# Rotary embedding on one core: casting loads and stores alternate in one ring, as DMAs of every fourth row

## Chip, core and metric

The kernel runs on 1 core of one Trainium2 chip. The metric is device time in microseconds (us), the median of several executions of the whole program. The profile is of one such execution.

## What is computed

The kernel rotates the two halves of every attention head by a position-dependent angle. x is float32 of 16 batches x 512 positions x 1024 values (16 heads of 64); cos and sin are float32 of 512 x 32.

```python
x = x.reshape(batch, seq, num_heads, head_dim)
x1, x2 = x[..., :half_dim], x[..., half_dim:]
cos = cos[None, :, None, :]
sin = sin[None, :, None, :]
rotated = np.concatenate([
    x1 * cos - x2 * sin,
    x1 * sin + x2 * cos
], axis=-1)
```

The result is float32 of the same size as x: 33.55 MB are read and 33.55 MB written.

## The kernel before

One batch is one unit of work: 512 positions x 1024 values, laid out as 128 partitions (rows of the tile) x 4096 values. Each partition holds four consecutive positions, which are contiguous in HBM, so a row is one run of 16 KB in float32. There are 16 batches, and for each the loop (L74 on) does four things.

- Load (L45 for the first three batches, L79 for the others): one DMA of 2 MB brings the batch to a float32 tile `xt`. It is issued on SP, on the queue that the profile calls hardware_dynamic. `xpool` has 4 buffers, so a load waits until ACT has cast the batch four before.
- Cast (L84): ACT copies `xt` to `xb` in bf16, 128x4096 in one instruction.
- Products and sum (L101, L102, L109): for each of the four positions of a partition, VectorE (DVE) multiplies `xb` with the cos table `cc` into `t1`, with the signed sin table `ss` into `t2`, and adds `t1` and `t2` with the halves of each head swapped into `ot`. All are bf16, 128x1024 each, 12 instructions per batch and 192 in all.
- Store (after L109, at L111): one DMA of 2 MB writes `ot` to the result. It is issued on POOL (GpSimd), on the software_dynamic queue, and casts bf16 to float32 on its way. `pool` has 3 buffers for each of its tiles, so a sum waits until the store of the batch three before is done.

Ahead of the loop cos and sin are loaded on POOL (L52, L55), and the tables are built by three short DVE operations (L67, L68, L72). The order of the instructions on each engine is the program's, with one exchange that the scheduler makes: DVE runs the products one position ahead of the sums. The waits follow from buffers and from data. In addition each DMA uses one of eight semaphores of its kind in turn, so that it waits for the eighth DMA of its kind before it.

Of the kernel before, what the change touches and what calls it, by code (L numbers as in the profile page):

```python
# [2 lines left out]

# [4 lines left out]


@with_exitstack  # L10
def kernel(
    ctx: ExitStack,
    tc: tile.TileContext,
    x: bass.AP,
    cos: bass.AP,
    sin: bass.AP,
    num_heads: int,
    out: bass.AP,
):
    nc = tc.nc  # L20
    P = nc.NUM_PARTITIONS

    batch, seq, dim = x.shape
    head_dim = dim // num_heads
    half = head_dim // 2

    out_flat = out.rearrange("b s h d -> b s (h d)")

    bf16 = mybir.dt.bfloat16
    f32 = mybir.dt.float32  # L30
    nh = num_heads
    hd = head_dim

    spp = seq // P
    W = spp * dim

    singles = ctx.enter_context(tc.tile_pool(name="singles", bufs=4))
    xpool = ctx.enter_context(tc.tile_pool(name="xpool", bufs=4))
    pool = ctx.enter_context(tc.tile_pool(name="pool", bufs=3))

    xts = {}
    prefetch = 3
    for b in range(prefetch):
        xt = xpool.tile([P, W], f32)
        nc.sync.dma_start(out=xt, in_=bass.AP(  # L45
            tensor=x.tensor, offset=x.offset + b * seq * dim,
            ap=[[W, P], [1, W]]))
        xts[b] = xt

    cos_sb = singles.tile([P, spp * half], f32)  # L50
    sin_sb = singles.tile([P, spp * half], f32)
    nc.gpsimd.dma_start(out=cos_sb, in_=bass.AP(  # L52
        tensor=cos.tensor, offset=cos.offset,
        ap=[[spp * half, P], [1, spp * half]]))
    nc.gpsimd.dma_start(out=sin_sb, in_=bass.AP(  # L55
        tensor=sin.tensor, offset=sin.offset,
        ap=[[spp * half, P], [1, spp * half]]))

    cc = singles.tile([P, spp * hd], bf16)
    ss = singles.tile([P, spp * hd], bf16)  # L60
    cos_src = dataclasses.replace(
        cos_sb, ap=[cos_sb.ap[0], [half, spp], [0, 2], [1, half]]
    )
    sin_src = dataclasses.replace(
        sin_sb, ap=[sin_sb.ap[0], [half, spp], [0, 2], [1, half]]
    )
    nc.vector.tensor_copy(out=cc, in_=cos_src)  # L67
    nc.vector.tensor_copy(out=ss, in_=sin_src)  # L68
    ss_neg = dataclasses.replace(
        ss, offset=ss.offset + half, ap=[ss.ap[0], [hd, spp], [1, half]]  # L70
    )
    nc.vector.tensor_scalar_mul(out=ss_neg, in0=ss_neg, scalar1=-1.0)  # L72

    for b in range(batch):  # L74
        if b in xts:
            xt = xts.pop(b)
        else:
            xt = xpool.tile([P, W], f32)
            nc.sync.dma_start(out=xt, in_=bass.AP(  # L79
                tensor=x.tensor, offset=x.offset + b * seq * dim,  # L80
                ap=[[W, P], [1, W]]))

        xb = pool.tile([P, W], bf16)
        nc.scalar.copy(out=xb, in_=xt)  # L84

        t1 = pool.tile([P, W], bf16)
        t2 = pool.tile([P, W], bf16)
        ot = pool.tile([P, W], bf16)

        for j in range(spp):  # L90
            xj = dataclasses.replace(xb, offset=xb.offset + j * dim,
                                     ap=[xb.ap[0], [1, dim]])
            cj = dataclasses.replace(cc, offset=cc.offset + j * hd,
                                     ap=[cc.ap[0], [0, nh], [1, hd]])
            sj = dataclasses.replace(ss, offset=ss.offset + j * hd,
                                     ap=[ss.ap[0], [0, nh], [1, hd]])
            t1j = dataclasses.replace(t1, offset=t1.offset + j * dim,
                                      ap=[t1.ap[0], [1, dim]])
            t2j = dataclasses.replace(t2, offset=t2.offset + j * dim,
                                      ap=[t2.ap[0], [1, dim]])  # L100
            nc.vector.tensor_mul(out=t1j, in0=xj, in1=cj)  # L101
            nc.vector.tensor_mul(out=t2j, in0=xj, in1=sj)  # L102
            t2_sw = dataclasses.replace(
                t2, offset=t2.offset + j * dim + half,
                ap=[t2.ap[0], [hd, nh], [-half, 2], [1, half]]
            )
            otj = dataclasses.replace(ot, offset=ot.offset + j * dim,
                                      ap=[ot.ap[0], [1, dim]])
            nc.vector.tensor_add(out=otj, in0=t1j, in1=t2_sw)  # L109

        nc.gpsimd.dma_start(out=bass.AP(  # L111
            tensor=out_flat.tensor, offset=out_flat.offset + b * seq * dim,
            ap=[[W, P], [1, W]]), in_=ot)


# [1 line left out]
_INS = ['x', 'cos', 'sin', 'num_heads']  # L117
_OUTS = [((16, 512, 16, 64), 'float32')]
#: Inputs that are plain numbers.
_NUMBERS = {'num_heads': 16}  # L120


# [26 lines left out]
```

## Time and profile before

| | us |
|---|---|
| median of 10 runs | 164.74 |
| lowest to highest | 164.57 to 164.94 |
| the profiled execution: time | 164.87 |
| the profiled execution: span | 163.1 |
| ACT cast of a batch, 128x4096 | 3.605 |
| DVE product or sum, 128x1024 | 0.68 (one starts every 0.60) |
| POOL issue of a store | 0.53 |
| load, from issue to landing | 35.0 (median) |
| store, from issue to landing | 21.7 (median) |

The span runs from the first to the last instruction on the core; the time also holds what lies around it. In the page of a profile, DVE, ACT and POOL have busy time and number of instructions. The row GB/s cuts the span into 40 equal slices and gives what the DMA engines moved in each. A queue's line has packets, MB, and the time of its packets as a share of 16 DMA engines' span; shares of two queues can add up to more than 100%, as packets of different queues overlap. A table by stretches has, for each, its length, the busy time of DVE, ACT and POOL with the number of instructions, the clock of an engine that is not used here, the busy share of the DMA engines, and GB/s. A line of waits names the engine and line that waited, what for, and the us in total, how often, and the longest. A load's 35 us to landing is mostly time spent behind other transfers in the queue, since several are issued ahead.

### The profile page before, as it was taken

How to read it: one execution, taken by the hardware profiler on the slowest of the kernel's cores; microseconds unless marked ns; L12 is line 12 of the kernel's file. 1: busy time of each engine (PE TensorE's matmuls, PEld its weight loads, DVE VectorE, ACT ScalarE, POOL GpSimd, SP SyncE). 2: the span in 40 equal slices, each digit the busy share in tenths (PEclk: the TensorE clock that was granted, in tenths of full speed). 3: DMA queues.
4: the chain of work that ended last, by engine and by line, in shares of the span. 5: the costliest groups of instructions: out<-in, count | busy, mean ns of one | idle time of the engine just before them, and what ended most of it. 6: DMA issues, size and time to landing. Idle time of an engine off the chain costs nothing.

```text
span 163.1 us, 344 instructions
## 1 busy us (share of the span) xinstructions
DVE 117.5 (72%) x195; ACT 59.0 (36%) x17; POOL 10.0 (6%) x22
## 2 busy tenths in 40 slices
DVE  0018999999689493976939589494976949899800
ACT  3077667080531707135080531707135080350000
POOL 3000010010101001010000101001010000101000
DMA  5999999999999999999999999999999999999993
GB/s 165 433 419 430 438 418 422 430 426 430 422 430 432 426 426 434 426 426 434 418 434 434 418 430 438 414 438 434 414 430 438 422 430 438 418 434 432 394 382 141
DMA packets 4674, 67.26 MB, mean 412 GB/s; under 512 B 544, under 2 KB 544, under 8 KB 576
## 3 DMA queue, kind: packets, MB, share of 16 engines
q1 hardware_dynamic: 2304, 33.56, 55.8%
q0 software_dynamic: 2368, 33.69, 49.8%
q14 instruction: 2, 0.02, 0.0%
HBM read 33.69 MB, written 33.55 MB: 412 GB/s over the span
## 4 chain that ended last, share of the span: by engine, by line
issue 60%; DMA 16%; DVE 13%; POOL 4%; ACT 2%; POOLq 0%; DVEq 0%
DMA out_dram<-ot 10%; DMA xt<-in_x_dram 5%; DVE ot L109 4%; DVE t L101 4%; DVE t L102 4%; POOL out_dram L111 4%; ACT xb L84 2%; POOLq L144 0%; POOLq L111 0%; DVEq L109 0%
## 5 line engine op out<-in xcount | busy, mean ns | idle before, releaser
L84 ACT CAST xb<-xt 128x4096 bf16<-128x4096 f32 x16 | 57.7, 3605 | 85.4 <-DMA xt<-in_x_dram 85.4
L109 DVE TENSOR_TENSOR ot<-t,t 128x1024 bf16<-128x1024 bf16 x64 | 43.8, 684 | 25.0 <-DMA out_dram<-ot 25.0
L101 DVE TENSOR_TENSOR t<-xb,cc 128x1024 bf16<-128x1024 bf16 x64 | 43.6, 682 | 3.1 <-ACT xb L84 3.1
L102 DVE TENSOR_TENSOR t<-xb,ss 128x1024 bf16<-128x1024 bf16 x64 | 43.7, 682 | 0.0
L111 POOL DMA_DIRECT2D out_dram<-ot x16 | 8.5, 533 | 144.3 <-DVE ot L109 144.3
L67 DVE CAST cc<-cos_sb 128x256 bf16<-128x256 f32 x1 | 0.3, 294 | 8.1 <-DMA cos_sb<-in_cos_dram 8.1
L84 ACT ACT_TABLE_LOAD x1 | 1.3, 1283 | 0.7 <-PEq L130 0.7
L68 DVE CAST ss<-sin_sb 128x256 bf16<-128x256 f32 x1 | 0.3, 293 | 0.7 <-DMA sin_sb<-in_sin_dram 0.7
L52 POOL DMA_DIRECT2D cos_sb<-in_cos_dram x1 | 0.7, 678 | 0.8 <-PEq L144 0.8
L55 POOL DMA_DIRECT2D sin_sb<-in_sin_dram x1 | 0.6, 557 | 0.0
L72 DVE TENSOR_SCALAR ss<-ss 128x128 bf16<-128x128 bf16 x1 | 0.2, 195 | 0.0
L130 POOL MEMSET const-float32-0.0<- 128x1 f32 x1 | 0.1, 99 | 0.2 <-issue 0.2
L130 POOL MEMSET const-bfloat16-1.0<- 128x1 bf16 x1 | 0.1, 102 | 0.0
L130 POOL MEMSET const-float32-1.0<- 128x1 f32 x1 | 0.1, 99 | 0.0
L130 POOL MEMSET const-uint8-127<- 128x1 uint8 x1 | 0.1, 99 | 0.0
## 6 DMA issues: line engine op xcount, KB each, us to landing
xt<-in_x_dram SPq DMA_DIRECT2D x16, 2048.0 KB, 35.0
out_dram<-ot POOLq DMA_DIRECT2D x16, 2048.0 KB, 21.7
cos_sb<-in_cos_dram POOLq DMA_DIRECT2D x1, 64.0 KB, 6.9
sin_sb<-in_sin_dram POOLq DMA_DIRECT2D x1, 64.0 KB, 7.2
```

The source lines that it names most:

```text
L52: nc.gpsimd.dma_start(out=cos_sb, in_=bass.AP(tensor=cos.tensor, offset=cos.offset, ap=[[spp * half, P], [1, spp * half]]))
L55: nc.gpsimd.dma_start(out=sin_sb, in_=bass.AP(tensor=sin.tensor, offset=sin.offset, ap=[[spp * half, P], [1, spp * half]]))
L67: nc.vector.tensor_copy(out=cc, in_=cos_src)
L68: nc.vector.tensor_copy(out=ss, in_=sin_src)
L72: nc.vector.tensor_scalar_mul(out=ss_neg, in0=ss_neg, scalar1=-1.0)
L84: nc.scalar.copy(out=xb, in_=xt)
L101: nc.vector.tensor_mul(out=t1j, in0=xj, in1=cj)
L102: nc.vector.tensor_mul(out=t2j, in0=xj, in1=sj)
L109: nc.vector.tensor_add(out=otj, in0=t1j, in1=t2_sw)
L111: nc.gpsimd.dma_start(out=bass.AP(tensor=out_flat.tensor, offset=out_flat.offset + b * seq * dim, ap=[[W, P], [1, W]]), in_=ot)
L130: nc = _bacc.Bacc("TRN2", target_bir_lowering=False, num_devices=1)
```

## The change

- x is loaded straight into a bf16 tile `xb` by casting DMAs that POOL issues on the software queue. The float32 tile and the cast on ACT are gone. SP issues only the loads of cos and sin.
- Each load and each store of a batch is four DMAs: DMA r moves the 32 partitions r, r+4, r+8 and so on, 512 KB in float32.
- Loads of three batches (12 DMAs) are issued first. Then, behind the sum of batch c, POOL issues store 0 of c, load 0 of c+3, store 1 of c, load 1 of c+3 and so on: the two kinds alternate in one ring. The last three batches have stores only.
- Products and sum of a batch are one instruction each of 128x4096 instead of four of 128x1024: 48 instead of 192.
- `xb` has 4 buffers, `t1` and `t2` 3, `ot` 4.
- The table `ss` is built by two operations from `sin_sb`, not by a copy and a change of sign in place.
- The eight semaphores are shared by loads and stores now, so each of these small DMAs waits for the eighth before it in the common order.

```diff
-    xts = {}
-    prefetch = 3
-    for b in range(prefetch):
-        xt = xpool.tile([P, W], f32)
-        nc.sync.dma_start(out=xt, in_=bass.AP(
-            tensor=x.tensor, offset=x.offset + b * seq * dim,
-            ap=[[W, P], [1, W]]))
-        xts[b] = xt
+    rows = 4
+    W = rows * dim
+    per_batch = spp // rows
+    nchunks = batch * per_batch
+    ahead = 3
+    pstep = 4
...
+    xpool = ctx.enter_context(tc.tile_pool(name="xpool", bufs=ahead + 1))
+    tpool = ctx.enter_context(tc.tile_pool(name="tpool", bufs=3))
+    opool = ctx.enter_context(tc.tile_pool(name="opool", bufs=4))
+    def view(t, offset, *dims):
+        return dataclasses.replace(t, offset=t.offset + offset,
+                                   ap=[t.ap[0], *[list(d) for d in dims]])
+    def dram(t, c, r):
+        b, k = divmod(c, per_batch)
+        return bass.AP(tensor=t.tensor,
+                       offset=t.offset + b * seq * dim + r * spp * dim + k * W,
+                       ap=[[pstep * spp * dim, P // pstep], [1, W]])
+    def load(c, r):
+        if r == 0:
+            xbs[c] = xpool.tile([P, W], bf16, tag="xb", name="xb")
+        nc.gpsimd.dma_start(out=xbs[c][r::pstep, :], in_=dram(x, c, r))
+    def store(c, r, ot):
+        nc.gpsimd.dma_start(out=dram(out_flat, c, r), in_=ot[r::pstep, :])
...
+    for t, src in ((cos_sb, cos), (sin_sb, sin)):
+        nc.sync.dma_start(out=t, in_=bass.AP(
...
+    for c in range(ahead):
+        for r in range(pstep):
+            load(c, r)
...
-        xb = pool.tile([P, W], bf16)
-        nc.scalar.copy(out=xb, in_=xt)
...
-        for j in range(spp):
...
-            nc.vector.tensor_mul(out=t1j, in0=xj, in1=cj)
-            nc.vector.tensor_mul(out=t2j, in0=xj, in1=sj)
...
-            nc.vector.tensor_add(out=otj, in0=t1j, in1=t2_sw)
-        nc.gpsimd.dma_start(out=bass.AP(
-            tensor=out_flat.tensor, offset=out_flat.offset + b * seq * dim,
-            ap=[[W, P], [1, W]]), in_=ot)
+        def tab(t):
+            return view(t, k * rows * hd, (hd, rows), (0, nh), (1, hd))
+        nc.vector.tensor_mul(out=t1, in0=xb, in1=tab(cc))
+        nc.vector.tensor_mul(out=t2, in0=xb, in1=tab(ss))
+        nc.vector.tensor_add(
+            out=ot, in0=t1, in1=view(t2, half, (hd, rows * nh), (-half, 2), (1, half)))
+        for r in range(pstep):
+            store(c, r, ot)
+            if c + ahead < nchunks:
+                load(c + ahead, r)
```

More of the change, by code (lines that the diff above doesn't have):

```diff
@@ L5 @@
 import concourse.tile as tile
-from concourse import bass_utils, mybir
+from concourse import bass_utils, masks, mybir
 from concourse._compat import with_exitstack
@@ L23 @@
     batch, seq, dim = x.shape
-    head_dim = dim // num_heads
-    half = head_dim // 2
-    out_flat = out.rearrange("b s h d -> b s (h d)")
+    nh = num_heads
+    hd = dim // nh
+    half = hd // 2
     bf16 = mybir.dt.bfloat16
     f32 = mybir.dt.float32
-    nh = num_heads
-    hd = head_dim
     spp = seq // P
[L35 to L39, printed above, removed]
@@ L41 @@
-    xts = {}
-    prefetch = 3
-    for b in range(prefetch):
-        xt = xpool.tile([P, W], f32)
-        nc.sync.dma_start(out=xt, in_=bass.AP(
-            tensor=x.tensor, offset=x.offset + b * seq * dim,
-            ap=[[W, P], [1, W]]))
-        xts[b] = xt
[L50 to L81, printed above, removed]
-        xb = pool.tile([P, W], bf16)
[L84 to L88, printed above, removed]
-        for j in range(spp):
[L91 to L100, printed above, removed]
-            nc.vector.tensor_mul(out=t1j, in0=xj, in1=cj)
-            nc.vector.tensor_mul(out=t2j, in0=xj, in1=sj)
[L103 to L109, printed above, removed]
-        nc.gpsimd.dma_start(out=bass.AP(
-            tensor=out_flat.tensor, offset=out_flat.offset + b * seq * dim,
-            ap=[[W, P], [1, W]]), in_=ot)
@@ new lines @@
+    rows = 4
[4 more added lines that the diff above has]
+    pstep = 4
+    BANK = 512
+    hpb = BANK // hd
+    out_flat = out.rearrange("b s h d -> b s (h d)")
+    singles = ctx.enter_context(tc.tile_pool(name="singles", bufs=1))
+    xpool = ctx.enter_context(tc.tile_pool(name="xpool", bufs=ahead + 1))
[4 more added lines that the diff above has]
+                                   ap=[t.ap[0], *[list(d) for d in dims]])
@@ new lines, in dram @@
+    def dram(t, c, r):
[3 more added lines that the diff above has]
+                       ap=[[pstep * spp * dim, P // pstep], [1, W]])
+    xbs = {}
+    def load(c, r):
[4 more added lines that the diff above has]
+        nc.gpsimd.dma_start(out=dram(out_flat, c, r), in_=ot[r::pstep, :])
@@ new lines @@
+    cos_sb = singles.tile([P, spp * half], f32, tag="cos_sb")
+    sin_sb = singles.tile([P, spp * half], f32, tag="sin_sb")
+    for t, src in ((cos_sb, cos), (sin_sb, sin)):
+        nc.sync.dma_start(out=t, in_=bass.AP(
+            tensor=src.tensor, offset=src.offset,
+            ap=[[spp * half, P], [1, spp * half]]))
+    for c in range(ahead):
+        for r in range(pstep):
+            load(c, r)
+    cc = singles.tile([P, spp * hd], bf16, tag="cc")
+    ss = singles.tile([P, spp * hd], bf16, tag="ss")
@@ new lines @@
+    nc.vector.tensor_copy(
+        out=cc, in_=view(cos_sb, 0, (half, spp), (0, 2), (1, half)))
+    sin_rows = view(sin_sb, 0, (half, spp), (1, half))
+    nc.vector.tensor_copy(
+        out=view(ss, 0, (hd, spp), (1, half)), in_=sin_rows)
+    nc.vector.tensor_scalar_mul(
+        out=view(ss, half, (hd, spp), (1, half)), in0=sin_rows, scalar1=-1.0)
+    for c in range(nchunks):
+        xb = xbs.pop(c)
+        k = c % per_batch
+        t1 = tpool.tile([P, W], bf16, tag="t1")
+        t2 = tpool.tile([P, W], bf16, tag="t2")
+        ot = opool.tile([P, W], bf16, tag="ot")
+        def tab(t):
[8 more added lines that the diff above has]
+                load(c + ahead, r)
```

## The prediction

> **What bounds the kernel now.** I read the engine shares first, then the row of transfer rates, the queues, the stretches, and last the waits.
>
> ```profile
> DVE 117.5 (72%) x195; ACT 59.0 (36%) x17; POOL 10.0 (6%) x22
> ...
> GB/s 165 433 419 430 438 418 422 430 426 430 422 430 432 426 426 434 426 426 434 418 434 434 418 430 438 414 438 434 414 430 438 422 430 438 418 434 432 394 382 141
> ...
> q1 hardware_dynamic: 2304, 33.56, 55.8%
> q0 software_dynamic: 2368, 33.69, 49.8%
> ...
> HBM read 33.69 MB, written 33.55 MB: 412 GB/s over the span
> ```
>
> No engine is full. The transfers are: between the second slice and the third from last the rate never leaves 394 to 438 GB/s. The counted bytes, 67.1 MB, are those of x in float32 plus those of the result in float32. A store reads only half that from SBUF (its source is bf16), so 67.1 MB counts each transfer by its wider side.
>
> ```profile
> 6.00:9.00 3.00, 0.29 (x1) 0.00 (x0) 0.00 (x0) 1.00 1.00 423
> 9.00:14.00 5.00, 1.70 (x5) 3.73 (x2) 0.00 (x0) 1.00 1.01 429
> ...
> 80.00:120.00 40.00, 30.09 (x51) 14.42 (x4) 2.13 (x4) 1.00 1.10 428
> ...
> 148.00:154.00 6.00, 5.96 (x11) 0.00 (x0) 0.53 (x1) 1.00 1.05 427
> ```
>
> The last column is GB/s. Loads alone (9 to 14 us) run at 429, loads beside stores (80 to 120) at 428, stores alone (148 to 154) at 427. So a casting store of 8 KB in and 16 KB out per row costs as much as a plain load of 16 KB in and 16 KB out. Its wider side sets its price, and loads and stores add up: 2,097,152 bytes at 428 GB/s is 4.90 us per batch and direction, 32 of them 156.8 us. The span is 163.1, so 6.3 us are ends: the first load is issued at 0.74 us and lands at 9.13, 3.5 us more than its 4.9 (4.2 us at the start), and 2.1 us remain at the end.
>
> ```profile
> ACT xb L84 <- DMA xt<-in_x_dram: 85.4, 16, 7.1
> DVE ot L109 <- DMA out_dram<-ot: 25.0, 11, 2.5
> ```
>
> ACT waits for loads and DVE for stores to free their buffers. Both are followers: what is worth time is bytes per transfer, or how well transfers overlap.
>
> **What the Trainium skill says.** "DMA: Bandwidth & Descriptors", section "SWDGE vs HWDGE vs iDMA": a casting transfer must be issued from GpSimd. The stores of before are such transfers, so the trace agrees as far as it goes; it shows no casting load. The same page, "Two DMAs through the same engine are not ordered": an engine's read and write sides are separate queues and descriptors of one queue are pipelined. If so, a read-heavy load can be read while a write-heavy store is still written. The trace of before can't confirm this, because its writes alone are 67.1 MB. "SBUF — State Buffer", "Who interferes with whom": descriptor generation on GpSimd is held up by one-input VectorE operations in a two-port mode, not by a two-input product. The trace agrees: the 16 store issues take 531 to 542 ns though DVE is running products around them.
>
> **Part 1: the cast leaves ACT and x is loaded as bf16.** ACT loses 16 casts of 3,605 ns, 57.7 us. In steady state they hide beside the transfers; the first is on the path to the first product (9.15 to 12.76 us), but transfers bound the run, so I give it no gain by itself. Bytes: reads stay 33.5 MB for x and 16.8 MB for the stores, together 50.3 MB; writes become 16.8 MB (x as bf16) plus 33.5, also 50.3 MB instead of 67.1. If each side runs at 428 GB/s and they overlap fully, a batch's store plus load costs 3/4 of 9.80 us, or 7.35 us. If each transfer still costs its wider side with no overlap, it remains 9.80. The trace can't tell: these are the two bounds.
>
> **Part 2: one ring, alternating, quarter transfers.** Each 2 MB transfer becomes four of 32 rows (512 KB, 1.225 us each by the wider side), store, load, store, load. Per such couple 2.45 us without overlap, 1.84 with all: up to 0.61 us to be had. To get it, an engine must read up to one 16 KB row ahead of its writes. Per engine 428/16 is 26.75 GB/s, or 612 ns per 16 KB row, and rows follow each other at that pace in the loads-only stretch, although the first row's delivery shows microseconds of lead. So reads must run ahead of writes by some part of a row. I take three quarters of the gain, 0.46 of 0.61, because some is lost at each change of direction: 1.99 us per couple before joints. Against it, more joints: 128 transfers of x and result where there were 32. A joint's price is at most what separates the measured 4.90 us per transfer from the 4.82 that the page's ceiling of 435 GB/s gives ("Where 436 GB/s comes from"), 0.08 us; at least nothing. I take joints as part of the unrecovered quarter, since both are small. Rounded between full overlap with 0.06 us per joint (7.35 + 8 x 0.06 = 7.83) and three quarters (7.96), a batch in the middle costs **7.8 us**; both are estimates.
>
> **Part 3: three loads lead, three stores trail.** Twelve quarter loads are issued first, without stores to pair with, and the last three batches' stores have no loads: 6 x 4.90 = 29.4 us at the unpaired price. Thirteen batches are paired: 13 x 7.8 = 101.4.
>
> **Part 4: issues move from SP to POOL.** POOL issues 64 loads and 64 stores; before it issued 18 transfers at 0.53 to 0.68 us. A 32-row issue lies between a quarter of 0.53 (0.13) and the whole 0.53 us; I take 0.5. Eight per batch are at most 4.3 us, beside 7.8 us of transfers, hidden; if the cover were gone, that is still less than the transfers. Each store waits on DVE's sum for its batch, and in POOL's order the load of the third batch ahead stands behind it. Each of these transfers also waits for the eighth one before it to finish, as compiled. Who suffers? A load L(c) lands when pair c-3 ends, at T. DVE is done with batch c by T + 2 (landing, as long as the 2.1 us of the end) + 6.6, and transfers of pairs c-2 and c-1 occupy the rings until T + 15.6. So the store is ready some 7 us early, and eight outstanding quarter transfers are 7.8 us of work, over the 3.5 us of lead. No new stall. At the start POOL's first issue was at 1.26 where SP's was at 0.74: **+0.5 us**. cos and sin move to SP, ahead of nothing; they gate only three short table operations before 9 us.
>
> **Part 5: larger DVE operations.** The 192 products and sums of 128x1024 become 48 of 128x4096. On the chain they start 0.602 us apart. "VectorE: DVE Perf Modes", "The TRN2 errata", prices a two-per-cycle operation at 58 cycles plus half the elements at 0.96 GHz: 594 ns for 1024, so trace and page agree within 2%. For 4096 that gives 2.19 us, against 4 x 0.602 = 2.41 as the upper bound. A batch is 6.6 us (7.2 at worst), all 16 105 us (116). It's under the 7.8 us of transfers, so it costs nothing; but it is next in line if transfers do better.
>
> **The sum.** 4.2 + 0.5 (start) + 14.7 (three loads) + 101.4 + 14.7 (three stores) + 2.1 (end) = 137.6 us of span. The profiled execution took 164.87 for a span of 163.1, so 1.77 lie around it; its time is 0.13 above the median of the ten runs (164.74). 137.6 + 1.8 - 0.1 = **139.3 us**.
>
> **The rivals.**
> - *Nearly no overlap* (middle case): reads run ahead by only a fifth to a quarter of what is needed, so a couple saves about 0.15 us. A pair is 9.2 us: 13 x 9.2 = 119.6, span 155.8, time **157.5 us**. For it: the busy share of mixed stretches in before is 1.10, so packets of two queues overlap by only a tenth. Against: those stretches had nothing to gain from reading ahead.
> - *Slower: each transfer keeps the price of its wider side, and the joints are paid.* Place: every engine's turn from one 32-row transfer to the next; price 0 to 0.08 us on 96 added joints, 0 to 7.7 us, with the 0.5 at the start. With 0.04: 164.7 + 0.5 + 3.8 = **169 us**, at most 173. It decides where the overlap saves less than about 0.33 us per pair (0.5 plus 3.8 us over 13 pairs). For it: every stretch shown costs transfers by adding wider sides, and no casting load has been seen. Against: separate sides as the skill tells.
> - *DVE becomes the bound*: the read side is faster than 428 or overlap is complete, and pairs fall below 6.6 us. Start 9.6 (first batch landed at 4.7 + 4.9), 105 of DVE, last store 4.9 plus about 3.5 as before: span 123, time **125 us**. Complete overlap at 7.35 lies between: 13 x 7.35 = 95.6, time 133.5.
> - *That it doesn't do what it says*: 32 rows that don't reach all 16 engines would halve the rate. The row step of four spreads them over the same rows as before, so I add it to the slower case.
>
> **Chances.** Forecast, with pairs of 7.3 to 8.6 us (132 to 150 us): 0.58. Nearly no overlap (150 to 164): 0.17. Slower: 0.17. DVE the bound (124 to 132): 0.08. Range: 126 to 158 leaves out the slower case and a sliver of the middle one, together 2 in 10. Within 0.2% (what a measurement of this kernel can tell from no change) lies only the edge between the cases, 0.02; so faster 0.81, slower 0.17. The forecast's own range is 132 to 150.
>
> **What would show it.** Pairs: from 40 to 80 us a batch is done every 7.8 us, so 5.1 batches or 15.4 large DVE operations in these 40 us, where the 51 small ones of before (80 to 120) are 4.25 batches. HBM reads plus writes over the span should come near 67 MB / 137 us, 490 GB/s, above the 438 that no slice of before exceeds. ACT empty; DVE at 105 us; DVE's idle time put down to loads. Wrong would be: a rate still at 428 in mixed stretches (no overlap), POOL issues near 1 us each or a POOL wait on DVE that leaves rings idle (the issue is the bound), or DVE operations above 2.4 us.

## The result, and the profile after

The changed kernel takes 170.77 us (median of 8 runs, 170.53 to 171.56) against 164.73 us for the kernel before (29 runs). The ratio is 1.0371, with a 95% interval of 1.0361 to 1.038: it is slower by 6 us. The profiled execution took 170.62 us for a span of 168.9. Four of the 11 executions of experiment 10 were slow ones of 168.9 us and are left out of its time and ratio.

The page of the changed kernel, the same lines as before:

```profile
DVE 109.1 (65%) x51; POOL 68.2 (40%) x132
...
GB/s 85 208 212 210 247 332 330 299 318 332 297 318 342 330 299 318 332 299 318 342 330 295 320 330 299 320 342 328 297 320 330 299 320 342 328 419 419 423 132 0
...
q0 software_dynamic: 6144, 50.34, 98.6%
q1 hardware_dynamic: 288, 0.13, 0.3%
...
HBM read 33.69 MB, written 33.55 MB: 398 GB/s over the span
```

The row GB/s needs care: it counts bytes on the side that is written. A casting load now counts 1 MB per batch where it reads 2. The 50.34 MB of q0 are 16.8 written to SBUF plus 33.5 written to HBM. The line for HBM counts both directions and fell from 412 to 398 GB/s over the span. Had the forecast been right, it would have risen to some 490.

The stretches (the last column is again GB/s, the one before it the busy share of the DMA engines; ACT has no work now and no column):

```profile
6.00:9.00 3.00, 0.00 (x0) 1.42 (x3) 1.00 0.99 205
9.00:14.00 5.00, 4.62 (x3) 0.53 (x1) 1.00 1.03 213
...
80.00:120.00 40.00, 27.58 (x13) 16.98 (x32) 1.00 1.05 319
...
148.00:154.00 6.00, 5.84 (x3) 0.53 (x1) 1.00 1.09 437
```

Casting loads alone (9 to 14 us) write 213 GB/s, so they read 426: the pace of the plain loads of before. Stores alone run at 437. In the mix, 319 GB/s written is 425 GB/s by the wider side (a batch writes 3 MB and has 4 MB by the wider side). Loads and stores still add up, and the DMA engines stay busy throughout (busy share 0.99 to 1.09 in these stretches). DVE shows the beat. Its first products of successive batches start like this:

```profile
39.61 2.29 DVE L100 TENSOR_TENSOR t<-xb,cc 128x4096 bf16<-128x4096 bf16 x1 [3.03 <-DMA xb<-in_x_dram]
...
49.46 2.29 DVE L100 TENSOR_TENSOR t<-xb,cc 128x4096 bf16<-128x4096 bf16 x1 [3.02 <-DMA xb<-in_x_dram]
...
59.32 2.29 DVE L100 TENSOR_TENSOR t<-xb,cc 128x4096 bf16<-128x4096 bf16 x1 [3.04 <-DMA xb<-in_x_dram]
```

A batch takes 9.86 us, where 7.8 was forecast and 9.79 was the period before (DVE's first products, 56.45 to 134.74 us, eight batches). DVE waits 3 us per batch for a load. So the middle gave nothing back, but it did not cost 6 us either. Most of those are at the end. The row GB/s ends in 132 and 0, where before it ended in 382 and 141. The waits of the queue on SP show what fills it; first the changed kernel, then the kernel before:

```profile
SPq L138 <- DMA out_dram<-ot: 161.2, 3, 158.8
SPq L138 <- PEq L138: 5.6, 2, 5.2
```

```profile
SPq L144 <- DMA out_dram<-ot: 55.9, 2, 46.6
SPq L144 <- PEq L144: 1.2, 2, 0.7
```

SP sees the last store landed at 163.1 us (161.7 before) and then waits 5.2 us more (0.7 before) at the barrier that ends the program. The line names PE, but PE has nothing to do in this kernel. The engine that was late is POOL, whose last DRAIN (the wait for its own work to be finished) lasts to the end; columns are duration in ns as min/median/max, then the first and last start:

```profile
L138 POOLq DRAIN  x3: 45/96/11648, 156.5 to 168.6; - x3
L138 SPq DRAIN  x3: 7/7/7, 163.1 to 168.4; - x3
```

The long one starts at 156.5 and ends 11.65 us later, at 168.2. The span grew by 5.8 us: 5.2 - 0.7 = 4.5 from this drain and 163.1 - 161.7 = 1.4 from the landing of the last store.

Two theories went into the experiments. Mine: transfers cost their wider side and don't overlap, and POOL's last drain costs 0.04 us for each software DMA (a DMA that POOL issues) (5.2/128 = 0.041 here, 0.7/18 = 0.039 before). Its rivals: that finer or coarser alternation wins overlap which something else eats, and that the late end comes with rows, packets or casting loads, not with the number of DMAs.

### The profile page after: what moved, and what is told of

It is laid out like the page before. It is cut to its first block, busy times and chain, and to the rows that moved or that the text cites. A ratio compares the mean times of both kernels' runs of the same rounds, so it can differ in the third digit from the quotient of the medians.

```text
span 168.9 us, 299 instructions
## 1 busy us (share of the span) xinstructions
DVE 109.1 (65%) x51; POOL 68.2 (40%) x132
## 3 DMA queue, kind: packets, MB, share of 16 engines
q0 software_dynamic: 6144, 50.34, 98.6%
## 4 chain that ended last, share of the span: by engine, by line
DMA 77%; DVE 7%; POOL 4%; issue 4%; POOLq 0%; DVEq 0%; PEldq 0%
DMA xb<-in_x_dram 77%; DVE ot L102 3%; DVE t L101 3%; POOL out_dram L66 2%; POOL xb L63 2%; DVE t L100 1%; POOLq L138 0%; DVEq L100 0%; DVEq L102 0%; PEldq L138 0%
## 5 line engine op out<-in xcount | busy, mean ns | idle before, releaser
L100 DVE TENSOR_TENSOR t<-xb,cc 128x4096 bf16<-128x4096 bf16 x16 | 36.7, 2291 | 42.6 <-DMA xb<-in_x_dram 42.4
L66 POOL DMA_DIRECT2D out_dram<-ot x64 | 34.2, 535 | 58.8 <-DMA out_dram<-ot 40.3
L63 POOL DMA_DIRECT2D xb<-in_x_dram x64 | 34.0, 532 | 30.1 <-DMA xb<-in_x_dram 29.1
L102 DVE TENSOR_TENSOR ot<-t,t 128x4096 bf16<-128x4096 bf16 x16 | 36.7, 2292 | 0.6
L101 DVE TENSOR_TENSOR t<-xb,ss 128x4096 bf16<-128x4096 bf16 x16 | 36.5, 2284 | 0.0
```

The lines of the kernel that those rows point to most:

```text
L63: nc.gpsimd.dma_start(out=xbs[c][r::pstep, :], in_=dram(x, c, r))
L66: nc.gpsimd.dma_start(out=dram(out_flat, c, r), in_=ot[r::pstep, :])
L100: nc.vector.tensor_mul(out=t1, in0=xb, in1=tab(cc))
L101: nc.vector.tensor_mul(out=t2, in0=xb, in1=tab(ss))
L102: nc.vector.tensor_add(out=ot, in0=t1, in1=view(t2, half, (hd, rows * nh), (-half, 2), (1, half)))
```

## Experiments

### 1. Whole transfers

```diff
-    pstep = 4
+    pstep = 1
```

> The changed kernel with whole transfers: each load and each store is one DMA of 128 rows (2 MB in float32), still casting, still alternating in one ring, so 32 software DMAs instead of 128. Theory (transfers don't overlap; the extra time is POOL's last drain, which costs 0.04 us for each software DMA issued): the middle stays at 9.8 us per batch, the last store lands as before, and the 5 us between landing and the end of the span shrink to about 1.3; time 166.4 us. Rival 1 (quartering does win some overlap that something else eats): a batch in the middle takes more than 9.85 us, time 171 us or more. Rival 2 (the late end is a matter of how many rows or packets were written, not of how many DMAs): the end stays over 3.5 us, time about 169 us.

Measured: 164.9 us, ratio to the kernel before 1.001 (1.0001 to 1.0018). A batch takes 9.73 us (ten batches between these two lines), less than the 9.86 of quarters:

```profile
48.88 2.29 DVE L100 TENSOR_TENSOR t<-xb,cc 128x4096 bf16<-128x4096 bf16 x1 [5.76 <-DMA xb<-in_x_dram]
...
146.14 2.29 DVE L100 TENSOR_TENSOR t<-xb,cc 128x4096 bf16<-128x4096 bf16 x1 [2.86 <-DMA xb<-in_x_dram]
```

The last store lands at 161.0 us, and the wait behind it is

```profile
SPq L138 <- PEq L138: 1.7, 2, 1.3
```

1.3 us, as expected for 32 DMAs. It is also not a matter of packets: this kernel has 4,608 packets on the software queue, the one of experiment 3 has 3,136 and a longer drain. Quartering the transfers is the whole loss: 3.9 us of drain and 2.1 us of earlier landing. Casting loads in POOL's ring without it are a draw with the kernel before, although ACT is idle. The time came out 1.5 us lower than expected because I had put the joints between transfers at nothing: a batch of quarters has six joints more and takes 0.14 us longer (9.865 against 9.726 before rounding), 0.023 us for each.

### 2. Every eighth row

```diff
-    pstep = 4
+    pstep = 8
```

> The changed kernel with DMAs of every eighth row: 16 rows each, one row per DMA engine, so 16 KB loads and stores alternate row by row; 256 software DMAs instead of 128. Theory (no overlap, 0.04 us of last drain per DMA): a batch in the middle stays at 9.85 to 10.0 us, the end grows from 5.1 to some 10 us, time 176 us. Rival 1 (reads can run ahead, but by less than the two rows of the quarter DMAs): a batch in the middle falls clearly below 9.85 us, to 9.2 or less, and DVE's idle time shrinks by 0.6 us per batch. Rival 2 (the late end goes with packets): the end grows less, to about 6.5 us, time 172 us.

Measured: 172.95 us, ratio 1.049 (1.0454 to 1.0526). Outside the pauses described below a batch takes 10.02 us (six batches between these two lines), not 9.2: with one 16 KB row per DMA engine and turn nothing overlaps either.

```profile
93.47 2.29 DVE L100 TENSOR_TENSOR t<-xb,cc 128x4096 bf16<-128x4096 bf16 x1 [5.48 <-DMA xb<-in_x_dram]
...
153.57 2.29 DVE L100 TENSOR_TENSOR t<-xb,cc 128x4096 bf16<-128x4096 bf16 x1 [3.21 <-DMA out_dram<-ot]
```

My theory of the end missed. The wait behind the last landing is 0.5 us, not 10. POOL lost time elsewhere, as its own rows of this kernel show:

```profile
81.33 0.48 POOL L63 DMA_DIRECT2D xb<-in_x_dram  x1
84.91 0.49 POOL L66 DMA_DIRECT2D out_dram<-ot  x1 [3.10 <-issue]
...
160.68 0.48 POOL L66 DMA_DIRECT2D out_dram<-ot  x1 [1.42 <-DVE ot L102]
164.03 3.34 POOL L66 DMA_DIRECT2D out_dram<-ot  x7 [2.87 <-issue]
```

POOL stood still for 3.1 us at 81.8 us and 2.9 us at 161.2 us with nothing to wait for. Up to the first pause it had issued 76 loads and 52 stores, 128 DMAs:

```profile
L63 POOL DMA_DIRECT2D xb<-in_x_dram x76: 481/481/713, 1.3 to 81.3; - x76
L66 POOL DMA_DIRECT2D out_dram<-ot x52: 489/489/537, 17.4 to 80.7; - x52
```

121 follow up to the second pause, and 7 after it. My reading is that bookkeeping for issued DMAs is put off until about 128 have gathered, or the program ends; the changed kernel has just 128 and would pay all at the end. The trace shows the pauses, not what POOL does in them, and 3.1 us for 128 DMAs is less than the 5.2 us of drain for 128, so this is not shown. The batch around the first pause takes 12.30 us (81.17 to 93.47). The second pause falls where the last stores wait to be issued and leaves the rings empty (16 GB/s at 163 to 164 us).

### 3. Quarter stores alone

```diff
-        nc.gpsimd.dma_start(out=bass.AP(
-            tensor=out_flat.tensor, offset=out_flat.offset + b * seq * dim,
-            ap=[[W, P], [1, W]]), in_=ot)
+        for r in range(4):
+            nc.gpsimd.dma_start(out=bass.AP(
+                tensor=out_flat.tensor, offset=out_flat.offset + b * seq * dim + r * W,
+                ap=[[4 * W, P // 4], [1, W]]), in_=ot[r::4, :])
```

> The kernel before, with one part of the change alone: each store is four DMAs of every fourth row; plain loads on SP, the cast on ACT and the small DVE operations stay. 66 software DMAs instead of 18. Theory: the transfers cost what they did, the last drain grows by 48 x 0.04 = 1.9 us; time 166.7 us. Rival (the late end comes with the casting loads or with the shared ring): no change, 164.7 us.

Measured: 167.23 us, ratio 1.0147 (1.0132 to 1.0163), 0.5 above the forecast (the last store lands at 162.1 us, not at 161.7), and the end as expected:

```profile
SPq L145 <- PEq L145: 3.2, 2, 2.7
```

2.7 us for 66 DMAs. No casting load is in this kernel and loads are in another ring, so the late end is not theirs.

### 4. Large DVE operations alone

Twelve operations of 128x1024 per batch become three of 128x4096, with the views of the changed kernel (its lines L97 to L103).

> The kernel before, with one part of the change alone: three DVE operations of 128x4096 per batch instead of twelve of 128x1024. Theory: transfers bound the middle, but behind the last load the cast, the sums and the last store stand in a row, and the rate falls to 279 GB/s at 154 to 157 us because the last store is issued late; DVE 0.3 to 0.6 us faster per batch (6.9 measured in the changed kernel against 7.2) over the last two batches brings the last store forward by up to 1 us: time 163.8 us. Rival: DVE is off the path altogether, 164.7 us.

Measured: 164.4 us, ratio 0.9976 (0.9965 to 0.9987). It lies between the two, nearer to the rival: the last store was issued at 154.17 us instead of 154.79, and the run gained 0.4 us. Experiments 7 and 10, which contain this part, end within 0.1 us of it, and their intervals overlap with its own; no other version that computes the whole result is faster than the kernel before.

### 5. Stores that don't cast

```diff
-        nc.gpsimd.dma_start(out=dram(out_flat, c, r), in_=ot[r::pstep, :])
+        dst = dram(out_flat, c, r)
+        dst = bass.AP(tensor=dst.tensor, offset=dst.offset,
+                      ap=[[pstep * spp * dim, P // pstep], [1, W // 2]])
+        nc.gpsimd.dma_start(out=dst, in_=ot.bitcast(f32)[r::pstep, :])
```

> The changed kernel, but its stores don't cast: each row writes its 8 KB of bf16 as they are (as 2048 float32 words) into the first half of the row's place, so half of the output is not written and the rest is not float32. The casting loads stay, and so do all 128 DMAs, their order and waits. It gives the stores the price that the forecast hoped for by overlap. Theory (a transfer costs its wider side, transfers add up): store 2.45 us and load 4.9 us per batch, a batch in the middle 7.4 us; L15 lands near 118 us, DVE 6.9 us, last store and its landing 3.5 us, last drain 5 us, time about 135 us; the steps of the forecast on POOL, waits and DVE hold at that pace. Rival 1 (a row has a price whatever its width): 9.85 us per batch, 171 us. Rival 2 (the eight outstanding DMAs, POOL or DVE would have bound it at that pace): 7.8 us or more per batch, with the rings idle between, 140 us or more.

Measured: 139.56 us, ratio 0.8478 (0.8465 to 0.8491). What it writes to HBM is halved, and its first products come faster:

```profile
HBM read 33.69 MB, written 16.78 MB: 367 GB/s over the span
```

```profile
50.37 2.29 DVE L103 TENSOR_TENSOR t<-xb,cc 128x4096 bf16<-128x4096 bf16 x1 [0.53 <-DMA xb<-in_x_dram]
...
57.77 2.29 DVE L103 TENSOR_TENSOR t<-xb,cc 128x4096 bf16<-128x4096 bf16 x1 [0.58 <-DMA xb<-in_x_dram]
```

A batch takes 7.39 us (43.03 to 116.88 us, ten batches): 8 KB in and 8 KB out costs half of 8 KB in and 16 KB out. That fits the price by the wider side, and shows that POOL's issues, the limit of eight outstanding DMAs and DVE would have carried the pace I had hoped for. It doesn't show that the wider side as such is what costs: the halved side is the one at HBM, and in every transfer of x and of the result in these runs the side at HBM is at least as wide as the other. Rival 2 named 140 us, near what was measured, but for another reason than the one seen: rings were not idle between batches. The 4.6 us over my 135 are mostly the end, where

```profile
SPq L141 <- PEq L141: 8.5, 2, 8.1
```

8.1 us stand where 128 DMAs should have cost 5.2. Here the last store landed only 2.6 us after the last issue had ended (128.7 against 126.1), in the changed kernel 5.7 us after (163.1 against 157.4).

### 6. Every eighth row, a second look

The kernel of experiment 2, unchanged.

> The changed kernel with DMAs of every eighth row once more, for a second look at where POOL pauses. Theory (POOL's bookkeeping of about 125 software DMAs at a time: put off to the end in kernels with fewer, 3 us in the middle here): pauses near 82 and 161 us again, each after about 125 DMAs, the last drain short. Rival (the pauses were chance): they lie elsewhere or are missing.

Measured: one run of 173.51 us, with pauses of 3.14 us at 81.8 and 2.87 us at 161.4 us, again at the same DMAs, and 0.5 us behind the last landing. The pauses are not chance.

### 7. Quartered last batches

```diff
+        n = spp if b < batch - 2 else 1
+        for j in range(0, spp, n):
+            lo, hi = j * dim, (j + n) * dim
+            nc.scalar.copy(out=xb[:, lo:hi], in_=xt[:, lo:hi])
...
-    nc.gpsimd.dma_start(out=cos_sb, in_=bass.AP(
+    nc.scalar.dma_start(out=cos_sb, in_=bass.AP(
```

> The kernel before with large DVE operations (as in the fourth experiment), the last two batches in four column quarters each (cast, products, sum and store of each position by itself), and the cos and sin loads issued on ACT; 22 software DMAs. Theory: 32 transfers at 4.9 us can't be shortened, only the gaps at the ends: 0.7 us between 149 and 156 us in which the rings wait for the last two stores go; the 4 more software DMAs cost 0.2 us; time 163.7 us. Rival (the gaps at the end are hidden by nothing else and come back as smaller transfers' own cost): 164.4 us, no change from large DVE operations alone.

Measured: 164.49 us, ratio 0.9982 (0.9975 to 0.9988). The rival holds: nothing beyond experiment 4. The rings were now full until 160 us, but the last store landed at 161.4 us, where experiment 4 has 161.2. Filling the gap did not bring the last landing forward; where the time went I did not trace.

### 8. Plain loads in the same ring

```diff
-            xbs[c] = xpool.tile([P, W], bf16, tag="xb", name="xb")
+            xbs[c] = xpool.tile([P, W], f32, tag="xt", name="xt")
...
-        xb = xbs.pop(c)
+        xt = xbs.pop(c)
+        xb = tpool.tile([P, W], bf16, tag="xb")
+        nc.scalar.copy(out=xb, in_=xt)
```

> The changed kernel with the cast of the loads undone alone: the same 64 + 64 quarter DMAs alternate in POOL's ring, but a load is float32 to float32 and ACT casts each batch in one instruction as before. Theory on the transfers (a row costs its wider side, 16 KB, with nothing overlapped): a batch in the middle 9.85 us, as with casting loads. Rival (the casting load was cheaper or dearer than a plain one): a batch differs by over 0.1 us. On the end, where the changed kernel had 5.2 us after the last landing for 128 DMAs and the raw-store kernel 8.1 for 128: if a DMA that doesn't cast costs POOL twice as much bookkeeping, the end is 8 us and the time about 174.5 us with 3.6 us for the last cast on the path; if what matters is how soon after the last issue the last store lands, the end is near 5 us and the time about 171.5 us.

Measured: 178.86 us, ratio 1.0849 (1.0824 to 1.0874). Where rings are full a batch takes 9.82 us (nine batches between these two lines; 9.89 with the three after them), against 9.86 with casting loads:

```profile
38.50 2.29 DVE L102 TENSOR_TENSOR t<-xb,cc 128x4096 bf16<-128x4096 bf16 x1 [3.21 <-ACT xb L93]
...
126.85 2.29 DVE L102 TENSOR_TENSOR t<-xb,cc 128x4096 bf16<-128x4096 bf16 x1 [2.97 <-ACT xb L93]
```

The loads write twice the bytes to SBUF, and the pace stays within 0.1 us: a load's cast on the way costs and saves nothing that these runs resolve. I had not expected the rest of the 8 us. The ring ran empty between 18 and 22 us (26 GB/s in the fifth slice) and again at 160 to 165 us (105 GB/s), because the cast on ACT (3.6 us, and before the first one 1.28 us for loading ACT's table) stands between the load and the sum:

```profile
POOL out_dram L66 <- DVE ot L104: 27.0, 4, 11.3
```

POOL waited 11.3 us for the first sum, and the next loads stood behind that store. In the changed kernel the same line has 6.4 as its longest. So the cast in the load does save something, a shorter chain, if loads and stores share one in-order ring. The wait behind the last landing is 6.0 us, here with landing 4.7 us after the last issue (171.1 against 166.4), so neither of the two guesses for the end held by itself. All three kernels with 128 DMAs fit one rule: POOL goes over them twice at 0.041 us each, once when its last issue is done (5.2 us), and once more when that and the last landing are past. For the changed kernel that gives 163.1 + 5.2 = 168.3, for this one 166.4 + 5.2 + 5.2 = 176.8, for experiment 5 126.1 + 10.4 = 136.5; measured 168.3, 177.1 and 136.8 (landing plus wait). The rule was made from these numbers and not tried on others, so it is a fit and no proof of a mechanism.

### 9. Half transfers

```diff
-    pstep = 4
+    pstep = 2
```

> The changed kernel with half transfers: DMAs of every second row, 64 rows each, 64 software DMAs. Theory (0.041 us of POOL's last drain for each software DMA): 2.6 us from the last landing to the end of the wait, between the 1.3 of 32 DMAs and the 5.2 of 128; time 166.5 us. Rival (the end grows in steps, when a ring has wrapped): either 1.3 us and 165 us or 5.2 us and 169 us.

Measured: 167.4 us, ratio 1.0158 (1.0132 to 1.0185), and

```profile
SPq L138 <- PEq L138: 3.0, 2, 2.6
```

2.6 us for 64 DMAs, as expected, with no steps. The time is 0.9 us above the forecast. The last store lands at 162.5 us, 1.5 later than with whole transfers. The joints explain some 0.4 us of it (9.76 against 9.73 us per batch, 13 batches); the rest I did not trace.

### 10. cos and sin behind the first load

```diff
+        if b == 0:
+            for t, src in ((cos_sb, cos), (sin_sb, sin)):
+                nc.sync.dma_start(out=t, in_=bass.AP(
...
```

> The kernel before with large DVE operations (as in the fourth experiment) and the loads of cos and sin put on SP between the first and the second load of x, so that nothing of theirs lies beside the first load; 16 software DMAs. In the kernel before the rate is 66 GB/s in the first 2 us and 246 in the next 2. Theory (32 transfers of 4.9 us cannot be shortened, but some of the 2.5 us lost in these 4 us goes to the small rows of cos and sin): time 163.9 us, first load landed at 8.5 us instead of 9.13. Rival (the start is the time to the first bytes, whoever is first): 164.4 us, no change from large DVE operations alone.

Measured: 164.49 us, ratio 0.9975 (0.9964 to 0.9985). The first load did land earlier (its cast starts at 8.60 us instead of 9.15), but the time is that of experiment 4: a start 0.5 us earlier in ACT's row did not move the rings' total.

## Why the prediction was wrong

The forecast was 139.3 us with a range of 126 to 158; measured were 170.77, slower than before and not faster. By its steps:

- **Overlap of reads and writes: this step failed.** "I take three quarters of the gain, 0.46 of 0.61": the gain is nil. A batch in the middle takes 9.86 us where the step gave 7.8; 13 batches make 26.8 us of the 31.3 between forecast and time. Alternation by whole transfers, halves, quarters and single rows gave 9.73, 9.76, 9.86 and 10.02 us: all near the 9.80 that the two wider sides cost at 428 GB/s, and none near the 7.35 of full overlap. The Trainium skill ("DMA: Bandwidth & Descriptors", "Two DMAs through the same engine are not ordered") says that the read and write sides are separate queues. These runs don't contradict that, but from separate queues I had concluded that a narrow side frees time for another transfer, and that doesn't follow. Why nothing is freed stays open: an engine may not read far enough ahead, a stage between both sides may pass the wider form, or the price may not go by the wider side at all but by the bytes at HBM, read and written together. Those are 67.2 MB before and after, so there would have been nothing to gain. Doubling the SBUF side of the loads changed nothing (experiment 8) and halving the HBM side of the stores halved their price (experiment 5), which fits the last reading as well as the first two. A transfer that is wider in SBUF than at HBM would tell them apart, and so might casting loads and stores in two rings; neither was run. The 7.8 itself lies below both figures, 7.83 and 7.96, that it is said to lie between, a slip of 2.1 us at most over 13 batches.
- **My argument for it** was that rows follow each other at 612 ns, so reads must run ahead of writes. That shows that latency is hidden; it does not show spare capacity. The busy share of 1.10 in mixed stretches, which I had set against the forecast and then put aside, pointed the right way, though it was no proof.
- **The end: a term that is missing.** I carried 2.1 us over from before. It is 7.0 from the last bytes on (about 161.9 us), 4.5 us of it more drain on POOL. "128 transfers of x and result where there were 32" was priced at joints on the rings alone; each issue also leaves work on POOL that comes due at the end (1.3, 2.6 and 5.2 us for 32, 64 and 128 DMAs, experiments 1 and 9 and the changed kernel).
- **Joints: right in kind.** Bounds 0 to 0.08 us, measured 0.023.
- **Start: near.** +0.5 was taken, and +0.2 came: the first product's wait ends at 9.3 us, where the first load of before landed at 9.13.
- **POOL's issues: hidden, as forecast.** 0.53 us for 128 rows (0.534) as for 32 (0.532), 0.49 for 16, near the 0.5 taken. Eight per batch are 4.3 us beside 9.86, and they stayed hidden beside 7.39 in experiment 5.
- **DVE: right.** An operation is busy for 2.29 us and one starts every 2.24, where the formula in the Trainium skill ("VectorE: DVE Perf Modes", "The TRN2 errata") gave 2.19 and four small ones 2.41. From first product to first product without a wait it is 6.73 us per batch, where 6.6 was taken.
- **The slower rival was right on its main point**, that loads and stores add up at full price. That its 169 us came near is in part luck: of its 3.8 us for joints, quarters cost 2.1 in landing against whole transfers, and the 4.5 us of drain, most of the loss, were not in it.

## What to carry to other kernels

Price a casting DMA by its wider side (here always the one at HBM) and add loads and stores up; an unused half of one side was not available to a neighbour in the same ring at any grain tried. Before cutting transfers into more software DMAs, count what each leaves behind: here 0.023 us in the ring and 0.04 us in POOL's last drain, so whole transfers were 5.9 us faster than quarters. Read the end of a program as a stage of its own: the time from the last landing to the end is a wait with an owner, and the owner need not be the engine that the line names.

## What was unexpected of the hardware

- After the last store has landed, the wait for POOL's drain goes on for 0.5 to 0.7 us with 16 to 22 software DMAs, 1.3 with 32, 2.6 with 64, 2.7 with 66 and 5.2 with 128, up to 8.1 where the last store lands soon after its issue.
- With 256 software DMAs POOL pauses for 3 us after 128 of them, and again after 121 more.
- A POOL issue of 128 rows costs what one of 32 does, 0.53 us.
- A casting load (16 KB read, 8 KB written per row) runs at the pace of a plain one: 426 GB/s of bytes read against 429.
